# Side-job weight pieces of a hybrid decoder layer on GpSimd's DMA queue instead of SyncE's

## The chip, the cores and the metric

The program runs on one core of one Trainium2 chip. The metric is the time of one execution on the device in microseconds; the shown time is the median of three executions. A profile of one further execution, with every instruction and every DMA packet, is read beside it.

## What is computed

One conditioned decoder layer over 256 tokens of width 2048, in float32. The part that matters here is the first line: a conditioning vector c is multiplied by a large matrix w_ada (2048 x 12288) and gives six vectors that shift, scale and gate the two halves of the layer.

```python
mod = jax.nn.silu(c) @ w_ada + b_ada
shift1, scale1, gate1, shift2, scale2, gate2 = jnp.split(mod[:, None, :], 6, axis=-1)
h = rms_norm(x, norm1_g) * (1.0 + scale1) + shift1
z = h @ w_in + b_in
...
mixed = (g_m[:, :, 0] * y_attn + g_m[:, :, 1] * y_conv) @ w_out
x = x + gate1 * mixed
h2 = rms_norm(x, norm2_g) * (1.0 + scale2) + shift2
return x + gate2 * peer_ffn(h2, peer_w_q, peer_sub_keys, peer_u, peer_v)
```

`y_attn` is a sparse attention with its own output projection, `y_conv` a convolution branch, and `peer_ffn` a product-key expert layer. Nearly all bytes are weights that are read once: 533 MB in 2.5 ms.

## The kernel before

The kernel is one long program for five engines that is written in the order in which TensorE works. **The weight stream** is its spine. A class `Stream` holds a plan of 512 KB chunks (tile `raw`, 128 x 1024, four buffers). `prefetch` issues a chunk's load on SyncE's DMA queue (line 149), ScalarE rounds each half chunk to a high part `hi` (line 153), and VectorE subtracts it to give a low part `lo` (line 159). One half chunk is a piece: `piece` lets TensorE do 12 matmuls of 128 x 256 with it (lines 200 to 202), with `hi` and `lo` made up to three to four pieces ahead (`AHEAD = 3`). A chunk's load can only be issued when the `lo` of the buffer's earlier chunk is done, so SyncE stands at such a wait much of the time.

**Side jobs** are Python generators. After each piece, `step` gives each running job `rate` steps (0.9 means nine steps in ten pieces); what a step emits goes into the engines' queues behind that piece. Two of them read w_ada:

- `ada_steps` (from 418 us to 925 us, beside the attention, the merge of the branches and the output projection) makes shift2, scale2 and gate1. It works through 12 groups of 512 columns, each of 16 pieces of 128 x 512 (256 KB, tile `adaw`, four buffers). Three pieces are asked for ahead; then every step asks for one more and VectorE adds one piece, scaled by c, onto an accumulator `ada` (lines 383 and 385). After the 16th, four steps follow without such a load: TensorE transposes the sums (line 390), ScalarE adds them over the columns (line 394). The rates are 0.7, 0.88, 0.9 and 0.94 in turn; 0.9 and 0.94 hold from the merge on.
- `gate2_steps` (2053 to 2403 us, beside the last expert products, rate 0.25) does the same with 64 pieces (tile `g2w`, line 1289).

Both ask for their pieces on SyncE's queue, so each such load stands in the program order of that queue between two chunks of the stream. GpSimd runs four small memsets at the start and then nothing. At 642 us the same queue also loads x again, one transfer of 2 MB (line 891).

Of the kernel before, what the change touches and what calls it, by code (L numbers as in the profile page):

```python
# [72 lines left out]
def build(nc, tc, d):  # L73
    ctx = ExitStack()
    ve, sc, pe, sp = nc.vector, nc.scalar, nc.tensor, nc.sync
# [34 lines left out]
    def v(name, i=0, n=1):  # L110
        o = VEC[name][0] + i
        return vec[:, o:o + n]
# [248 lines left out]
    def ada_steps(groups, bank):  # L361

        pool = adap[0]
        todo = [(g, k) for g in groups for k in range(KT)]
        ahead = []

        def load():
            if todo:
                g, k = todo.pop(0)
                raw = pool.tile([128, 512], F32, name="adaw", tag="adaw", bufs=4)  # L370
                sp.dma_start(raw, d["w_ada"][k * 128:(k + 1) * 128, (g - 8) * 512:(g - 7) * 512])
                ahead.append(raw)

        for _ in range(3):
            load()
        yield
        for g in groups:
            acc = pool.tile([128, 512], F32, name="ada", tag="ada", bufs=2)
            for k in range(KT):
                load()  # L380
                raw = ahead.pop(0)
                if k == 0:
                    ve.tensor_scalar(acc, raw, sc_c[:, 0:1], None, op0=OP.mult)
                else:
                    ve.scalar_tensor_tensor(acc, raw, sc_c[:, k:k + 1], acc, op0=OP.mult, op1=OP.add)  # L385
                yield
            yield
            ps = bank()
            for j in range(4):
                pe.transpose(ps[:, j], acc[:, j * 128:(j + 1) * 128], ident)  # L390
            yield
            cols = mod[:, 4 * g:4 * g + 4]
            for j in range(4):
                sc.activation(acc[:, j * 128:(j + 1) * 128], ps[:, j], AF.Copy, accum_out=cols[:, j:j + 1])
            yield
            ve.tensor_add(cols, cols, v("b_ada", 4 * g, 4))
            yield
# [881 lines left out]
    def gate2_steps():  # L1279

        todo = [(g, k) for g in range(4) for k in range(KT)]
        ahead = []

        def load():
            if todo:
                g, k = todo.pop(0)
                raw = vp.tile([128, 512], F32, name="g2w", tag="g2w", bufs=4)
                o = D * 3 + g * 512
                sp.dma_start(raw, d["w_ada"][k * 128:(k + 1) * 128, o:o + 512])
                ahead.append(raw)  # L1290

        ve.memset(gacc, 0.0)
        sp.dma_start(gacc[0:1], d["b_gate2"])
        for _ in range(3):
            load()
        yield
        for g in range(4):
            for k in range(KT):
                load()
                a = gacc[:, g * 512:(g + 1) * 512]  # L1300
                ve.scalar_tensor_tensor(a, ahead.pop(0), sc_c[:, k:k + 1], a, op0=OP.mult, op1=OP.add)
                yield
# [130 lines left out]
```

## Time and profile before

| | |
|---|---|
| median of three executions | 2494.17 us (2492.91 to 2499.4) |
| the profiled execution | 2496.72 us, span of its instructions 2494.9 us |
| TensorE busy in that span | 2448.4 us (98%) |
| VectorE, ScalarE busy | 1942.8 us (78%), 1422.5 us (57%) |
| mean granted TensorE clock | 0.995 |
| DMA | 540 MB, 217 GB/s on the mean |

The span runs from the first to the last instruction. A busy share counts time in which at least one instruction of an engine is in work. In views of waits, "A <- B" reads: A stood idle, and the last thing that it waited for was B.

### The profile page before, as it was taken

To read this page: it belongs to the slowest core of one execution; us is meant where nothing else is said; L and a number is where in the kernel's file an instruction comes from. 1 tells how busy PE (TensorE), PEld (TensorE's weight loads), DVE (VectorE), ACT (ScalarE), POOL (GpSimd) and SP (SyncE) were. 2 spreads that over 40 slices of the span, in tenths; PEclk is the share of its full clock that TensorE was granted. 3 is DMA by queue.
4 is the path that set the end of the run, shared out by engine and by line. 5 is a ranking of instruction groups with operands and counts; after the bars stand their busy time and mean duration, and the time that the engine had idled before them with its cause. 6 is when DMAs were issued, how large, how long until landed. Compare 5 with 4: busy or idle time off the path is not lost.

```text
span 2494.9 us, 44063 instructions
## 1 busy us (share of the span) xinstructions
PE 2448.4 (98%) x15324; PEld 2168.3 (87%) x15324; DVE 1942.8 (78%) x4136; ACT 1422.5 (57%) x3198; POOL 0.2 (0%) x4
## 2 busy tenths in 40 slices
PE   7999999999999999999999999999999999999999
PEld 6899999888999899988888888888888888888887
DVE  7979886888787786899997888888655556666665
ACT  1045456776444456555568888887555555555554
POOL 0000000000000000000000000000000000000000
PEclk9999999999999999999999999999999999999999
DMA  9955556655898885555555555555555557777765
GB/s 376 401 195 194 179 191 200 200 156 189 304 296 281 278 292 194 178 191 191 189 189 178 177 177 174 175 177 178 186 193 190 192 193 254 237 242 240 236 209 194
DMA packets 171553, 540.48 MB, mean 217 GB/s; under 512 B 18753, under 2 KB 19009, under 8 KB 171073
## 3 DMA queue, kind: packets, MB, share of 16 engines
q1 hardware_dynamic: 171330, 537.67, 64.5%
q8 instruction: 120, 1.97, 0.3%
q14 instruction: 103, 0.84, 0.1%
HBM read 533.41 MB, written 4.19 MB: 215 GB/s over the span
## 4 chain that ended last, share of the span: by engine, by line
PE 88%; DVE 6%; DMA 5%; issue 1%; SPq 0%; ACT 0%; DVEq 0%
PE ps_acc L213 19%; PE ps_acc L217 9%; PE acc L200 7%; PE acc L202 7%; PE acc L201 7%; DMA adaw<-in_w_ada_dram 4%; DVE acc L309 3%; PE ps_o L1314 2%; PE ps_s L1314 2%; PE ps_t L1314 2%; PE ps_acc L1314 2%; PE ps_o L1313 2%; PE ps_s L1313 2%; PE ps_t L1313 2%; PE ps_acc L1313 2%; PE ps_o L1312 2%
## 5 line engine op out<-in xcount | busy, mean ns | idle before, releaser
L153 ACT CAST hi<-raw 128x512 fp32r<-128x512 f32 x1548 | 952.2, 620 | 808.2 <-PE acc L201 236.8
L159 DVE TENSOR_TENSOR lo<-raw,hi 128x512 fp32r<-128x512 f32 x1548 | 1062.9, 688 | 385.2 <-PE ps_o L1313 78.6
L213 PE MATMUL ps_acc<-h,hi 128*128 128x512 f32 x2048 | 564.6, 397 | 0.0
L213 PEld LDWEIGHTS ps_acc<-h,hi 128*128 128x128 f32 x2048 | 346.7, 188 | 44.2
L217 PEld LDWEIGHTS ps_acc<-h,lo 128*128 128x128 f32 x2048 | 311.4, 188 | 46.4
L200 PE MATMUL acc<-hhi,hi 128*128 128x256 f32 x1200 | 346.9, 289 | 0.0
L202 PE MATMUL acc<-hhi,lo 128*128 128x256 f32 x1200 | 334.7, 279 | 4.3 <-DVE lo L159 4.3
L201 PE MATMUL acc<-hlo,hi 128*128 128x256 f32 x1200 | 334.0, 278 | 0.0
L217 PE MATMUL ps_acc<-h,lo 128*128 128x256 f32 x2048 | 318.0, 277 | 0.0
L200 PEld LDWEIGHTS acc<-hhi,hi 128*128 128x128 f32 x1200 | 226.0, 188 | 6.3 <-issue 5.3
L202 PEld LDWEIGHTS acc<-hhi,lo 128*128 128x128 f32 x1200 | 226.1, 188 | 5.4 <-DVE lo L159 5.3
L201 PEld LDWEIGHTS acc<-hlo,hi 128*128 128x128 f32 x1200 | 226.0, 188 | 3.2 <-issue 3.1
L385 DVE SCALAR_TENSOR_TENSOR ada<-adaw,sc_c,ada 128x512 f32<-128x512 f32 x180 | 134.6, 748 | 49.9 <-DMA adaw<-in_w_ada_dram 49.6
L1204 ACT ACTIVATE Ahi<-ohA,high 128x128 f16<-128x128 f16 x256 | 100.7, 393 | 10.8 <-PE ps_o L1225 10.6
L471 DVE SCALAR_TENSOR_TENSOR cacc<-glu,dwh,cacc 128x256 f32<-128x256 f32 x240 | 105.7, 479 | 0.0
L341 PE MATMUL zb<-hr,w 128*128 128x256 f32 x448 | 101.3, 385 | 0.0
L1204 ACT ACTIVATE Alo<-ohA,low 128x128 f16<-128x128 f16 x256 | 99.0, 387 | 0.0
L341 PEld LDWEIGHTS zb<-hr,w 128*128 128x128 f32 x448 | 85.6, 194 | 11.4
L309 DVE SCALAR_TENSOR_TENSOR acc<-wa,sc_c,acc 128x256 f32<-128x256 f32 x224 | 91.3, 478 | 0.0
L202 PE MATMUL acc<-ohi,lo 128*128 128x256 f32 x256 | 74.2, 290 | 5.2 <-DVE lo L159 4.8
L202 PE MATMUL acc<-mhi,lo 128*128 128x256 f32 x256 | 73.9, 288 | 1.5 <-DVE lo L159 1.5
L201 PE MATMUL acc<-mlo,hi 128*128 128x256 f32 x256 | 73.2, 286 | 1.0 <-DVE mlo L907 1.0
(367 smaller groups left out, 4406.0 us busy)
## 6 DMA issues: line engine op xcount, KB each, us to landing
raw<-in_u_dram SPq DMA_DIRECT2D x256, 512.0 KB, 3.6
raw<-in_v_dram SPq DMA_DIRECT2D x256, 512.0 KB, 4.5
raw<-in_w_in_dram SPq DMA_DIRECT2D x150, 512.0 KB, 4.4
adaw<-in_w_ada_dram SPq DMA_DIRECT2D x192, 256.0 KB, 5.4
wa<-in_w_ada_dram SPq DMA_DIRECT2D x64, 512.0 KB, 8.8
raw<-in_nsa_out_dram SPq DMA_DIRECT2D x32, 512.0 KB, 5.3
raw<-in_w_out_dram SPq DMA_DIRECT2D x32, 512.0 KB, 5.2
raw<-in_peer_wq_dram SPq DMA_DIRECT2D x32, 512.0 KB, 3.7
```

The lines of the kernel that those rows point to most:

```text
L153: sc.copy(hi, self.source(n))
L159: ve.tensor_sub(lo, self.source(n), hi.bitcast(F32))
L200: pe.matmul(ps, hi[:, o:o + 128], xhi[:, k], start=(k == 0), stop=False)
L201: pe.matmul(ps, hi[:, o:o + 128], xlo[:, k], start=False, stop=False)
L202: pe.matmul(ps, lo[:, o:o + 128], xhi[:, k], start=False, stop=(k == nk - 1))
L213: pe.matmul(ps.rearrange("p a t -> p (a t)"), hi[:, o:o + 128], x[:, k].rearrange("p a t -> p (a t)"), start=(k == 0), stop=False)
L217: pe.matmul(ps[:, 1], lo[:, o:o + 128], x[:, k, 0], start=False, stop=(k == nk - 1))
L309: ve.scalar_tensor_tensor(a, raw[:, i], c, a, op0=OP.mult, op1=OP.add)
L341: pe.matmul(zb[n // 2][:, n % 2], ws[k][n // 7][:, n % 7], hr[k], start=(k == 0 and n % 2 == 0), stop=(k == KT - 1), skip_group_check=True)
L1204: sc.activation(part[:, j], A[:, j], AF.Copy, scale=g[:, t0 + j:t0 + j + 1])
L1313: pe.matmul(ps, chi, lo, start=False, stop=False)
L1314: pe.matmul(ps, clo, hi, start=False, stop=(i1 == NK - 1))
```

## The change

The two lines that issue the pieces of w_ada for the side jobs name another engine's queue. Nothing else is different.

```diff
@@ ada_steps @@
                 raw = pool.tile([128, 512], F32, name="adaw", tag="adaw", bufs=4)
-                sp.dma_start(raw, d["w_ada"][k * 128:(k + 1) * 128, (g - 8) * 512:(g - 7) * 512])
+                nc.gpsimd.dma_start(raw, d["w_ada"][k * 128:(k + 1) * 128, (g - 8) * 512:(g - 7) * 512])
                 ahead.append(raw)
@@ gate2_steps @@
                 o = D * 3 + g * 512
-                sp.dma_start(raw, d["w_ada"][k * 128:(k + 1) * 128, o:o + 512])
+                nc.gpsimd.dma_start(raw, d["w_ada"][k * 128:(k + 1) * 128, o:o + 512])
                 ahead.append(raw)
```

The rows of TensorE, VectorE and ScalarE stand in the same order as before. On SyncE's queue in the merge, before, around the load of x (`x_7756`), the pieces `adaw` stand between the stream's chunks `raw`:

```order
L149 DMA raw<-in_w_in_dram 128x1024
L371 DMA adaw<-in_w_ada_dram 128x512
L149 DMA raw<-in_nsa_out_dram 128x1024
L891 DMA x_7756<-in_xT_dram 128x4096
L149 DMA raw<-in_nsa_out_dram 128x1024
L149 DMA raw<-in_w_in_dram 128x1024
L371 DMA adaw<-in_w_ada_dram 128x512 x2
L149 DMA raw<-in_w_in_dram 128x1024
L371 DMA adaw<-in_w_ada_dram 128x512 x2
```

The same place of SyncE's queue in the changed kernel:

```order
L149 DMA raw<-in_w_in_dram 128x1024 x2
L149 DMA raw<-in_nsa_out_dram 128x1024
L891 DMA x_7756<-in_xT_dram 128x4096
L149 DMA raw<-in_nsa_out_dram 128x1024
L149 DMA raw<-in_w_in_dram 128x1024 x2
L149 DMA raw<-in_nsa_out_dram 128x1024 x2
```

The chunks and the load of x keep their order, and nothing stands between them any more. GpSimd's queue, in the changed kernel, from the program's start, with what each row waits for (`DMASW` and `DMAHW` are completions of DMAs of GpSimd's and SyncE's queue, `DVE` is VectorE's progress):

```order
L1424 MEMSET const-uint8-127 128x1
L1429 UNCONDITIONAL_BRANCH [waits barrier_Pool_Activation_PE_DVE_SP_gather]
L371 DMA adaw<-in_w_ada_dram 128x512 [waits DMAHW3_49,DMAHW4_49,DMAHW1_49,DMAHW5_49,DVE_49,Activation_49]
L371 DMA adaw<-in_w_ada_dram 128x512 x3
L371 DMA adaw<-in_w_ada_dram 128x512 [waits DMASW0_49,DVE_49]
L371 DMA adaw<-in_w_ada_dram 128x512 [waits DMASW1_49,DVE_49]
L371 DMA adaw<-in_w_ada_dram 128x512 [waits DMASW2_49,DVE_49]
```

All 192 loads of `adaw` and then the 64 of `g2w` moved here. The first waits for the memory under its buffer, which the program's first stage uses; the next three wait for nothing; from the fifth on each waits for an earlier load and for VectorE's use of the buffer, and for no chunk of the stream.

## Rows read from the trace of the kernel before

**Rows 1.** Page, first line
```profile
span 2494.9 us, 44063 instructions
```
**Rows 2.** Busy time by stretch; columns in the second line
```profile
core 0: us, PE busy (x) PEld busy (x) DVE busy (x) ACT busy (x) POOL busy (x), PEclk, DMA share, GB/s
...
620.00:700.00 80.00, 76.86 (x625) 75.37 (x625) 60.76 (x104) 38.34 (x82) 0.00 (x0) 0.96 0.87 297
700.00:740.00 40.00, 37.80 (x321) 36.78 (x321) 33.37 (x57) 18.94 (x40) 0.00 (x0) 1.00 0.93 301
740.00:930.00 190.00, 175.48 (x1439) 171.74 (x1437) 150.58 (x263) 91.78 (x211) 0.00 (x0) 0.98 0.88 284
930.00:1040.00 110.00, 110.00 (x930) 109.65 (x929) 81.47 (x191) 67.20 (x135) 0.00 (x0) 1.00 0.58 194
2050.00:2400.00 350.00, 350.00 (x1531) 287.18 (x1530) 240.60 (x382) 177.67 (x319) 0.00 (x0) 1.00 0.73 240
```
**Rows 3.** Waits of TensorE, 620 to 930 us: us, times, longest
```profile
PE acc L202 <- DVE lo L159: 10.4, 11, 2.7
PE ps_t L390 <- DVE ada L385: 8.1, 6, 2.1
```
**Rows 4.** Waits of VectorE, 620 to 930 us
```profile
DVE ada L385 <- DMA adaw<-in_w_ada_dram: 49.2, 47, 5.5
```
**Rows 5.** Waits of VectorE, 700 to 930 us
```profile
DVE ada L385 <- DMA adaw<-in_w_ada_dram: 35.5, 39, 2.2
```
**Rows 6.** Timeline of VectorE: start, us, instruction, idle before and its end
```profile
700.92 0.75 DVE L385 SCALAR_TENSOR_TENSOR ada<-adaw,sc_c,ada 128x512 f32<-128x512 f32 x1 [1.31 <-DMA adaw<-in_w_ada_dram]
701.59 0.69 DVE L159 TENSOR_TENSOR lo<-raw,hi 128x512 fp32r<-128x512 f32 x1
...
709.11 0.75 DVE L385 SCALAR_TENSOR_TENSOR ada<-adaw,sc_c,ada 128x512 f32<-128x512 f32 x1 [0.37 <-DMA adaw<-in_w_ada_dram]
```
**Rows 7.** Timeline of SyncE's queue at the same place
```profile
702.30 0.33 SPq L149 DMA_DIRECT2D raw<-in_w_in_dram  x1
702.68 0.91 SPq L371 DMA_DIRECT2D adaw<-in_w_ada_dram  x2
```
**Rows 8.** Line 371, 700 to 930 us: issues in ns, and landing
```profile
L371 SPq DMA_DIRECT2D adaw<-in_w_ada_dram x100: 327/423/684, 702.7 to 919.1; - x100
...
DMA to landing us min/median/max: 4.5/5.8/7.3
```
**Rows 9.** Line 371, two loads that were issued singly
```profile
L371 SPq DMA_DIRECT2D adaw<-in_w_ada_dram x1: 431/431/431, 710.9 to 710.9; - x1
...
DMA to landing us min/median/max: 4.5/4.5/4.5
...
L371 SPq DMA_DIRECT2D adaw<-in_w_ada_dram x1: 424/424/424, 722.2 to 722.2; - x1
...
DMA to landing us min/median/max: 5.1/5.1/5.1
```
**Rows 10.** Tile adaw over the whole span
```profile
L371 SPq DMA_DIRECT2D adaw<-in_w_ada_dram x192: 327/423/1667, 418.2 to 919.1; - x192
...
L383 DVE TENSOR_SCALAR ada<-adaw,sc_c x12: 478/482/486, 423.0 to 895.5; 128x512 f32<-128x512 f32 x12
```
**Rows 11.** Tile g2w, 64 loads of the same size: landing
```profile
DMA to landing us min/median/max: 2.8/5.0/8.6
```
**Rows 12.** Line 149, 700 to 930 us: who waited for chunks, and landing
```profile
  ACT hi L153: 8.1, 6
...
DMA to landing us min/median/max: 3.9/5.2/7.0
```
**Rows 13.** Timeline of SyncE's queue around the load of x
```profile
642.65 0.42 SPq L891 DMA_DIRECT2D x<-in_xT_dram  x1
...
647.54 1.68 SPq L371 DMA_DIRECT2D adaw<-in_w_ada_dram  x2
```
**Rows 14.** Timeline of VectorE after it
```profile
657.42 0.75 DVE L385 SCALAR_TENSOR_TENSOR ada<-adaw,sc_c,ada 128x512 f32<-128x512 f32 x1 [5.50 <-DMA adaw<-in_w_ada_dram]
```

## The prediction

> **What bounds the kernel now.** I read the busy time by stretch first. TensorE is without a gap from 930 to 1040 us and in the last expert products from 2050 to 2400 us, but not in the merge and the output projection, from 620 to 930 us [rows 2]. There it stands idle for 80 - 76.86 = 3.1, 40 - 37.80 = 2.2 and 190 - 175.48 = 14.5 us, together 19.9 us. In two of the three stretches its granted clock is also below 1, so for a part of the time it ran at the lower of its two levels (1.2 GHz for 2.4): 0.96 over 80 us and 0.98 over 190 us are 3.2 + 3.8 = 7.0 us of full clock lost. The stake is therefore 26.9 us, 1.1% of the time; everywhere else that the change touches, TensorE has nothing to get back.
>
> Next the waits there. TensorE waits for VectorE alone: for `lo` of the stream, and, at a group's end, for the accumulator `ada` [rows 3]. VectorE in turn has one large wait, for the pieces `adaw`: 49.2 us in 47 waits [rows 4]. It works in order, so while it stands at an `ada` whose piece has not landed, the `lo` behind it is late too, and with it TensorE.
>
> The timelines tell why a piece is late. The buffer that VectorE frees at 700.92 + 0.75 = 701.67 us is the next piece's [rows 6]. But SyncE first has a chunk to issue, and that waits for the `lo` that ends at 701.59 + 0.69 = 702.28; the chunk goes at 702.30, the piece at 702.68, 1.01 us after its buffer was free [rows 7]. A second piece goes right behind it. The first is used at 709.11, after 0.37 us of idle time: 6.4 us under way. Over 100 loads the median landing is 5.8 us [rows 8], while two that were issued singly took 4.5 and 5.1 [rows 9], mean 4.8: the chunk and the twin ahead on the queue cost about a microsecond more.
>
> With four buffers the loop of one buffer is: freed, issued, landed, used. Before, that is 1.01 + 5.8 + 0.75 = 7.56 us for four steps. TensorE's own pace comes from the undisturbed stretch: 110 us for 930 matmuls are 0.118 us each, 1.42 us for a piece of 12 [rows 2], and at a mean rate of 0.92 steps a piece 1.42 / 0.92 = 1.54 us a step, 6.2 us for four. The loop is 1.36 us too long. In a group of 16 pieces with three asked for ahead, the 4th, 8th, 12th and 16th pay it: 5.4 us. The trace has 35.5 us of this idle time between 700 and 930 us [rows 5], and 100 loads [rows 8] are 6.25 groups: 5.7 us a group, so the loop explains it. TensorE's idle time there is 16.7 us, 2.7 a group. So about 3.0 us a group stay hidden in the three pieces of lead and in the four steps without a load.
>
> **What the change removes.** The wait of `adaw` behind chunks and the issue of the twin: 1.01 us for the first of a pair. VectorE's, ScalarE's and TensorE's rows are the same, so what is left on SyncE is the stream alone; its chunks lose the pieces ahead of them. The 256 issues of 0.42 us leave that queue [rows 10]; SyncE waits for `lo` anyway, so I cost this at nothing.
>
> **What it adds.** GpSimd issues 256 loads. It does nothing else, so nothing is queued behind them but the next load. The trace has no DMA from GpSimd, so its extra time per load from free buffer to landing, call it p, has to be bounded. Below: 0, as quick as SyncE. Above: 2.8 us, one more of the shortest landings of a transfer of this size [rows 11], as if the issue cost as much as the whole transfer. SyncE's own issues of this shape take 0.42 us at the median and 1.67 at the longest [rows 10]; I take the middle of these, p = 1.0.
>
> **What it moves.** GpSimd does not follow the order of the stream. At a group's end, where the program asks for nothing during four steps, it loads as soon as a buffer is free. So four pieces, not three, wait at a group's start, and only the 5th, 9th and 13th pay. It also loads the first four pieces long before 418 us, where TensorE has hardly a gap; I count nothing for that. The pieces of `g2w` are off the path with either queue, as TensorE is busy for 350.00 of 350 us there [rows 2]: nothing to gain or to lose.
>
> At the load of x, 2 MB go onto the queue at 642.65, two pieces behind it at 647.54 [rows 13], and VectorE stands for 5.50 us [rows 14]. On a queue of their own the pieces are not behind x in order, only beside it. This is part of the stake above.
>
> **The sum.** The new loop is p + 4.8 + 0.75 = 5.55 + p, with the single loads' landing since pieces no longer go in pairs behind a chunk. With p = 1.0 it is 6.55 us, 0.35 too long, times three 1.1 us a group, under the 3.0 that stay hidden. By this the whole stake would come back. But groups differ (one wait of 5.5 us beside many of about 1), and at full pace TensorE asks for more bytes than the 284 to 301 GB/s with DMA engines 0.88 to 0.93 busy [rows 2], so landings will not all be 4.8. I keep a third of the stake as lost: 26.9 x 2/3 = 18 us. The profiled execution took 2496.72 us (span 2494.9 [rows 1] and 1.8 around it) and would come to 2478.7; it lies 2.55 us over the median of the runs, so I forecast **2476 us**.
>
> The ends: with p = 0 the loop is 5.55 us, inside 6.2, and the whole stake comes back: 2494.2 - 26.9 = 2467. With p = 1.67, 7.22 us, 1.02 x 3 = 3.1 a group, still about hidden, but any scatter shows; half the stake, 2481. With p = 2.8, 8.35 us, 2.15 x 3 = 6.5 a group, 0.75 more than the 5.7 of today; with 135 loads or 8.4 groups after 620 us that is 6.3 us, and 7.0/19.9 more for the clock, 8.5 in all: 2503. The change turns to a loss where 3 x (p + 5.55 - 6.2) exceeds 5.7, at p = 2.55.
>
> The Trainium skill ("DMA: Bandwidth & Descriptors", section "Specifications") gives a first byte after about 1 us on GpSimd's path and about 0.6 us on SyncE's. By that, as an estimate, p is 0.4 and the sum the full stake, 2467. No run here shows it.
>
> **Rivals.** *No change: the queue was not the limit.* All transfers share the same 16 DMA engines, busy for 0.87 to 0.93 of these stretches against 0.58 behind them [rows 2]. If landings stay at 5.8 us because the engines are full, the new loop is 1.0 + 5.8 + 0.75 = 7.55, as long as the old; three payments instead of four are left as a gain, against chunks that now lose turns to the pieces. Chunks land after 5.2 us at the median and 7.0 at most, against some six pieces or 8.5 us between a buffer's release and the next rounding, and ScalarE already waits 8.1 us for them [rows 12]. The two about cancel: 2490, within 2487 to 2501. Against it speaks that single loads in the same stretch land in 4.8. Beside this stands the Trainium skill's "DMA: Bandwidth & Descriptors", section "Issuing engines are not separate DMA queues": transfers of all issuing engines interleave on the same engines, and a second issuer saves only issue time. The trace shows one queue, so it neither agrees nor disagrees.
>
> *Slower: GpSimd's issue itself is long.* Its place is between a freed buffer and the first byte, 192 times in a row. From p = 2.55 on it decides; 2.8 gives 2503.
>
> *Slower by more: VectorE holds GpSimd's issue up.* If GpSimd could prepare a transfer only while VectorE is idle, which is 190 - 150.58 = 39 of 190 us or 0.21 [rows 2], 1.0 us of issue would stretch to 4.8; the loop would be 10.35, 4.15 x 3 = 12.5 us a group, 6.8 more than today, 57 us in 8.4 groups and 20 for the clock: 2571. Nothing in the trace speaks for it or against it.
>
> The Trainium skill's "SBUF — State Buffer" ("Who interferes with whom") has such a lock, but only for VectorE's two-port modes, and says that a tensor_tensor has none. By that only the 12 scalings of 0.482 us, in the shape of [rows 10], could hold a transfer up, 6 us in all and most of them hidden.
>
> **How the numbers follow.** I give the forecast (2466 to 2487) 0.60, no change (2487 to 2501) 0.18, the long issue (2501 to 2510) 0.12, the lock (above 2510) 0.10. About 0.3%, 7.5 us, is what a measurement of this kernel can tell from no change; so faster has 0.60, same 0.18, slower 0.22. The range for 8 in 10 is 2466 to 2505: it leaves out a few hundredths below and about 0.15 above. The likeliest case's own range is 2466 to 2487.
>
> **What would show it.** Right: `adaw` loads start within about 0.1 us of the end of the use four before, no longer 1.0; landing counted from there below 6 us; VectorE's wait for `adaw` after 620 us under 20 us instead of 49; TensorE's idle time in 620 to 930 us under 8 us, and its clock at 1.00; the first four loads at about 140 us. Wrong: GpSimd's issues of 2.5 us or more in a row; a wait of ScalarE for chunks of well over 8 us in its place; `lo` or `ada` instructions of VectorE longer than 0.69 and 0.75 us, which would mean that the two engines disturb each other; or any change of TensorE's idle time outside 418 to 930 us.

## The result, and the profile after

The changed kernel takes **2467.28 us** (median of four, 2465.55 to 2469.65). The kernel before took 2493.54 us on the same chip (2491.16 to 2499.4). The ratio is 0.9889, with a 95% interval of 0.9875 to 0.9902: 26 us faster by the medians. The forecast of 2476 us, made from 2494.17, is a ratio of 0.9927 and lies outside this interval. The time is at the foot of the range (2466 to 2505) and at the value given for an issue that costs nothing (2467).

The profiled execution took 2467.69 us. The page's first lines, which answer to [rows 1]:

```profile
span 2465.9 us, 44212 instructions
...
PE 2432.3 (99%) x15324; PEld 2156.2 (87%) x15324; DVE 1941.6 (79%) x4136; ACT 1423.4 (58%) x3198; POOL 139.4 (6%) x260
```

Busy time by stretch, the columns as in [rows 2]:

```profile
418.00:470.00 52.00, 52.00 (x429) 49.80 (x427) 43.21 (x96) 33.05 (x99) 8.59 (x16) 1.00 0.68 224
620.00:700.00 80.00, 79.31 (x688) 78.72 (x687) 68.22 (x117) 40.86 (x89) 21.49 (x40) 1.00 0.93 328
700.00:740.00 40.00, 38.63 (x341) 38.44 (x340) 34.93 (x62) 21.19 (x51) 10.20 (x19) 1.00 0.93 322
740.00:930.00 190.00, 186.01 (x1581) 185.05 (x1580) 158.29 (x278) 105.78 (x233) 40.28 (x75) 1.00 0.87 300
```

TensorE's idle time in the three stretches of the stake fell from 19.9 us to 0.69 + 1.37 + 3.99 = 6.05 us, and the granted clock is at full speed in all of them (it was 0.96, 1.00 and 0.98). More bytes move per second there (300 to 328 GB/s for 284 to 301), since the same work is done in less time.

The waits of three engines from 620 to 930 us (us, times, longest), which answer to [rows 3, 4]:

```profile
DVE ada L385 <- DMA adaw<-in_w_ada_dram: 22.4, 33, 1.9
ACT hi L153 <- DMA raw<-in_w_in_dram: 13.4, 12, 2.1
ACT hi L153 <- DMA raw<-in_nsa_out_dram: 8.3, 7, 2.5
...
PE ps_t L390 <- DVE ada L385: 4.7, 3, 2.5
...
PE acc L202 <- DVE lo L159: 0.8, 3, 0.5
```

VectorE's wait for the pieces halved (49.2 to 22.4 us). TensorE's wait for `lo`, which stood behind it, nearly vanished (10.4 to 0.8), and that for `ada` at a group's end went from 8.1 to 4.7. The longest wait, 5.5 us at the load of x, is gone; the longest is now 1.9.

One loop of a buffer in the timelines, first VectorE's rows, then GpSimd's:

```profile
720.04 0.75 DVE L385 SCALAR_TENSOR_TENSOR ada<-adaw,sc_c,ada 128x512 f32<-128x512 f32 x1
```
```profile
721.08 0.54 POOL L371 DMA_DIRECT2D adaw<-in_w_ada_dram  x1 [1.17 <-DVE ada L385]
```

The use ends at 720.79, the load is issued at 721.08, 0.29 us later. This replaces the 1.01 us of [rows 6, 7], and here no chunk and no twin stand between. Line 371 from 700 to 930 us (durations of the issues in ns), which answers to [rows 8]:

```profile
L371 POOL DMA_DIRECT2D adaw<-in_w_ada_dram x94: 536/538/545, 700.7 to 888.8; - x94
...
  DVE ada L385: 17.0, 25
...
DMA to landing us min/median/max: 3.8/5.5/7.5
```

**Where the time came from.** Both programs give TensorE the same instructions in the same order, so the start of its n-th instruction can be compared between the two traces. Of the 29.0 us between the two profiled executions, 25.5 came in 620 to 930 us. 1.15 us came at 418 us, where the first four pieces, loaded at 137 us, are now waiting for VectorE. Another 1.9 us came between 150 and 200 us, in the first stage. That step is there too in e2_gate_only below, which leaves `adaw` where it was, and missing in e4_pool_five, which has the change; so it belongs to the single execution, and the medians differ by 26.3 us. The rest, some 0.5 us, came in small parts before 418 us. From 930 us to the end nothing came or went, the stretch of gate2 included.

### The profile page after: what moved, and what is told of

Same layout as the page of the kernel before. It is cut to its first block, busy times and chain, and to the rows that moved or that the text cites. A ratio compares the mean times of both kernels' runs of the same rounds, so it can differ in the third digit from the quotient of the medians.

```text
span 2465.9 us, 44212 instructions
## 1 busy us (share of the span) xinstructions
PE 2432.3 (99%) x15324; PEld 2156.2 (87%) x15324; DVE 1941.6 (79%) x4136; ACT 1423.4 (58%) x3198; POOL 139.4 (6%) x260
## 4 chain that ended last, share of the span: by engine, by line
PE 88%; DVE 6%; DMA 3%; issue 2%; POOL 0%; SPq 0%; ACT 0%; DVEq 0%; POOLq 0%
PE ps_acc L213 19%; PE ps_acc L217 10%; PE acc L200 8%; PE acc L202 7%; PE acc L201 7%; DVE acc L309 3%; DMA adaw<-in_w_ada_dram 3%; PE ps_o L1312 2%; PE ps_s L1312 2%; PE ps_t L1312 2%; PE ps_o L1314 2%; PE ps_s L1314 2%; PE ps_acc L1312 2%; PE ps_t L1314 2%; PE ps_acc L1314 2%; PE ps_o L1313 2%
## 5 line engine op out<-in xcount | busy, mean ns | idle before, releaser
L385 DVE SCALAR_TENSOR_TENSOR ada<-adaw,sc_c,ada 128x512 f32<-128x512 f32 x180 | 134.4, 746 | 22.9 <-DMA adaw<-in_w_ada_dram 22.4
L371 POOL DMA_DIRECT2D adaw<-in_w_ada_dram x192 | 104.8, 546 | 784.1 <-DVE ada L383 333.5
L1289 POOL DMA_DIRECT2D g2w<-in_w_ada_dram x64 | 34.3, 537 | 1429.3 <-ACT hi L153 864.7
L1204 ACT ACTIVATE Ahi<-ohA,high 128x128 f16<-128x128 f16 x256 | 100.7, 393 | 10.9 <-PE ps_o L1225 10.7
L200 PE MATMUL acc<-mhi,hi 128*128 128x256 f32 x256 | 73.2, 286 | 0.0
```

The costliest lines, as they stand in the source:

```text
L200: pe.matmul(ps, hi[:, o:o + 128], xhi[:, k], start=(k == 0), stop=False)
L1204: sc.activation(part[:, j], A[:, j], AF.Copy, scale=g[:, t0 + j:t0 + j + 1])
```

## The experiments

My theory ahead of them: a buffer's loop (freed, issued, landed, used) was longer than the four steps it may take, and the change shortens it by issuing as soon as the buffer is free. The rivals: the queue of its own is worth something by itself; or running ahead at group ends does it; or gate2's pieces or GpSimd's path have a part. All times are medians beside runs of the kernel before on the same chip.

| run | us | kernel before | ratio, 95% |
|---|---|---|---|
| e1_ada_only | 2470.34 | 2496.80 | 0.9898 (0.9879 to 0.9917) |
| e2_gate_only | 2495.26 | 2496.80 | 0.9994 (0.9984 to 1.0003) |
| e3_sync_five | 2467.01 | 2493.04 | 0.9889 (0.9872 to 0.9905) |
| e4_pool_five | 2461.21 | 2493.04 | 0.9874 (0.9857 to 0.9890) |
| e5_pool_coupled | 2529.49 | 2496.80 | 1.0135 (1.0114 to 1.0155) |
| e6_pool_delay | 2481.53 | 2493.04 | 0.9947 (0.9931 to 0.9964) |
| e7_pool_delay2 | 2496.91 | 2496.80 | 1.0001 (0.9987 to 1.0014) |
| e8_act_queue | 2470.69 | 2493.04 | 0.9902 (0.9886 to 0.9919) |
| e9_coupled_pad | 2495.27 | 2495.67 | 1.0000 (0.9990 to 1.0009) |
| e10_shift | 2526.18 | 2495.67 | 1.0122 (1.0105 to 1.0139) |
| e11_ahead_only | 2492.62 | 2495.67 | 0.9982 (0.9971 to 0.9992) |
| e12_early_only | 2473.03 | 2495.67 | 0.9905 (0.9888 to 0.9921) |

### Each half of the change alone: e1_ada_only, e2_gate_only

The first moves only `adaw` to GpSimd's queue, the second only `g2w`.

> Only the adaw loads go to GpSimd's queue, the g2w loads stay with SyncE. Theory (the whole gain comes from adaw, which no longer waits behind chunks of the stream): 2467 us, the same as the full change, within 0.2%. Rival (relieving SyncE's queue helps wherever it is done, gate2 too): between 2470 and 2485.

> Only the g2w loads go to GpSimd's queue. Theory: 2494 us, no change, as TensorE has no gap from 2050 to 2400 us. Rival: a part of the gain, some 5 to 10 us, or a loss of some us if GpSimd's issues disturb VectorE there.

The pieces of `adaw` alone give 0.9898, within the interval of the full change. Its 2470.34 us also touch the foot of the rival's range (2470 to 2485), so the other half decides: the pieces of `g2w` give nothing. Under gate2, TensorE stays without a gap in e2_gate_only, as in [rows 2]:

```profile
2050.00:2400.00 350.00, 350.00 (x1531) 287.20 (x1530) 240.56 (x383) 177.73 (x318) 32.19 (x60) 1.00 0.73 236
```

### A longer loop allowed, without any other queue: e3_sync_five; and with it: e4_pool_five

Both have five buffers instead of four, and four pieces asked for ahead. The memory comes from a second buffer of `mr`, a tile of the merge. The first keeps all loads on SyncE's queue, the second has the change as well.

```diff
-                raw = pool.tile([128, 512], F32, name="adaw", tag="adaw", bufs=4)
+                raw = pool.tile([128, 512], F32, name="adaw", tag="adaw", bufs=5)
...
-        for _ in range(3):
+        for _ in range(4):
...
-            mr = tp.tile([128, T], F32, name="mr", tag="mr", bufs=2)
+            mr = tp.tile([128, T], F32, name="mr", tag="mr", bufs=1)
```

> The kernel before with all loads on SyncE's queue, but five adaw buffers and four pieces asked for ahead (the memory comes from the tile mr, one buffer instead of two). Theory of the loop: 7.56 us now stand against five steps, 7.7 us, so the waits nearly go without any change of queue: 2465 to 2472. Rival (the pieces' place on SyncE's queue itself is what costs, or the DMA engines are full): 2480 to 2494.

> The changed kernel with five adaw buffers and four pieces asked for ahead. Theory: a loop of 6.5 us against 7.7, so the 6 us that TensorE still stands idle between 620 and 930 us go too: 2460 to 2463. Rival (the DMA engines, 0.87 to 0.93 busy, set the pace by now): 2466 to 2469, with longer landings.

One more buffer on the old queue has the whole gain of the change (0.9889 both). The pieces are then issued as late as before and land later, after 6.3 us at the median, but they have five steps for it (line 371, 700 to 930 us):

```profile
L371 SPq DMA_DIRECT2D adaw<-in_w_ada_dram x95: 327/425/1582, 702.4 to 887.6; - x95
...
DMA to landing us min/median/max: 4.6/6.3/7.4
```

From the end of a use to the issue it is 0.80 us on the mean, and the loop is 0.80 + 6.30 + 0.75 = 7.85 us, about the five steps of 7.7 that the expectation named; of the 34.0 us that e4_pool_five wins in 620 to 930 us, 6.9 stay lost. From 930 us on, TensorE's instructions in both runs go at the pace of the kernel before to 0.02 us, so the smaller `mr` costs nothing there.

With both edits TensorE has no gap left from 620 to 930 us (here the last stretch of e4_pool_five, and VectorE's wait, which was 49.2 us):

```profile
740.00:930.00 190.00, 190.00 (x1623) 190.00 (x1622) 163.06 (x291) 112.58 (x243) 39.70 (x74) 1.00 0.87 301
```
```profile
DVE ada L385 <- DMA adaw<-in_w_ada_dram: 2.1, 4, 1.3
```

This has the lowest median of the kernels run. Its interval overlaps that of the changed kernel (0.9857 to 0.9890 beside 0.9875 to 0.9902), but by TensorE's instructions it gained 34.0 us in 620 to 930 us, 8.5 more than the changed one. With no gap and full clock left, 34.0 us is what there was to win; the changed kernel took 25.5 of it.

### The issue made late again: e6_pool_delay, e7_pool_delay2

GpSimd fills the buffer with zeros before it issues the load, once or twice, which adds time between the free buffer and the issue and leaves the queue its own.

```diff
+                nc.gpsimd.memset(raw, 0.0)
                 nc.gpsimd.dma_start(raw, d["w_ada"][k * 128:(k + 1) * 128, (g - 8) * 512:(g - 7) * 512])
```

> The changed kernel, but GpSimd fills each adaw buffer once with zeros before it issues the load: some 0.5 to 0.8 us more between free buffer and landing. Theory of the loop: 7.1 to 7.3 us, about 3 us a group, just at what stays hidden: 2470 to 2477. Rival (only the four pieces at a group's start count): 2467 to 2469.

> The changed kernel, but GpSimd fills each adaw buffer twice with zeros once it is free, before it issues the load: a dearer issue, some 1 to 1.5 us more between free buffer and landing. Theory of the loop (6.5 us in the changed kernel against 6.2, three payments a group, 3.0 us hidden): 7.8 us, 1.6 x 3 = 4.8 us a group, about 1.8 us of it on TensorE, 8.4 groups and the clock: 2482 to 2490. Rival (the length of the issue does not matter, four pieces that wait at a group's start are the whole gain): 2467 to 2471.

e6_pool_delay kept less than half of the gain, e7_pool_delay2 none; both lost more than expected. GpSimd's timeline in e6_pool_delay shows the delay: 0.53 us of work and 0.30 us until the issue.

```profile
716.70 0.53 POOL L371 MEMSET adaw<- 128x512 f32 x1 [0.24 <-DVE ada L386]
717.52 0.54 POOL L372 DMA_DIRECT2D adaw<-in_w_ada_dram  x1 [0.30 <-POOL adaw L371]
```

So a loop that is half a microsecond longer costs more than half of the gain (11.6 us are left of 25.5 in 620 to 930 us): the loop has hardly any room.

The run also limits what the early issue explains. On the mean its loads go out 0.95 us after the buffer is free, later than the 0.78 of the kernel before, and yet the 11.6 us are kept. What is left in its favour is that it runs ahead at a group's end and that its loads land after 5.40 us instead of 5.79; how much each of the two is worth was not separated.

### GpSimd's queue, coupled to the stream: e5_pool_coupled, e9_coupled_pad; and what disturbed the first: e10_shift

Before each load GpSimd copies one element of the `lo` for which SyncE would have waited there, so that the load stands behind a chunk's `lo` again, but on a queue of its own. The copy goes into a new tile `touch`, of 4 bytes in e5_pool_coupled.

```diff
+    touch = const.tile([128, 1], F32, name="touch")
...
+                lo = S.parts.get(2 * S.loaded - 9)
+                if lo is not None:
+                    nc.gpsimd.tensor_copy(touch, lo[1][:, 0:1].bitcast(F32))
```

> The changed kernel, but GpSimd reads one element of the stream's latest lo before each adaw load, so that the load waits for what it waited for on SyncE and cannot run ahead at a group's end; the DMA queue stays its own. Theory (going ahead of the stream is what counts): from free buffer to issue about 1 us again for the first of two, the loop 0.7 us longer than in the changed kernel (7.2 to 7.5 us), four payments a group, VectorE's wait for adaw back to 40 to 50 us and the time to 2485 to 2495. Rival (a queue of its own is what counts, as pieces no longer stand behind a chunk): 2467 to 2472, with the wait near 20 us.

It came out slower than the kernel before, by 33 us, which no theory had. TensorE's instructions show why this says little: in 620 to 930 us it is within 2 us of the kernel before, and the 33 us are lost in every other stage from 200 us on (4.3 from 1040 to 1300 us, 4.7 from 1300 to 1640). The tile moves every buffer allocated after it by 4 bytes. e10_shift is the kernel before with that tile alone, written once; e9_coupled_pad is e5_pool_coupled with a tile of 256 bytes.

> The kernel before with one more buffer of 4 bytes a partition, written once with zeros, ahead of nearly all other buffers; queues and order unchanged. Theory (the 4 bytes cost what the coupled run lost outside 620 to 930 us, about 33 us): 2520 to 2530. Rival (the 4 bytes cost nothing, the coupled run lost it by its reads): 2494.

> As the coupled run (GpSimd reads one element of the stream's latest lo before each adaw load), but the target of that read is a buffer of 256 bytes a partition in place of 4, so that the buffers allocated after it keep their alignment. Theory (going ahead of the stream is the gain, and what the coupled run lost outside 620 to 930 us came from buffers that lay 4 bytes off): no loss outside that stretch, the gain inside it gone, 2488 to 2498 us. Rival (the reads themselves disturb VectorE or TensorE): 2520 to 2530 again.

e10_shift lost 30 us by 4 bytes of memory (below, in the last section), stage by stage nearly what e5_pool_coupled lost outside 620 to 930 us. With 256 bytes the loss is gone and e9_coupled_pad is as fast as the kernel before. Its stretch looks like that of [rows 2]:

```profile
740.00:930.00 190.00, 175.94 (x1422) 171.50 (x1421) 149.78 (x261) 90.61 (x210) 76.77 (x160) 0.97 0.85 282
```

So a queue of its own gives nothing when the issue is held behind the stream and made later by a copy. The reserve matters: within a group the loads of e9_coupled_pad went out 1.22 us after the buffer was free, on the mean, for 0.78 before, and landed after 5.48 us for 5.79, so that the whole loop is about the old one. A coupled load with the old delay wasn't run; if it landed as soon, the rule in the table below would give it some 10 us (an estimate: 0.78 + 5.48 + 0.75 = 7.01 us against 7.32). That the queue alone is worth nothing is therefore not shown.

### Another queue: e8_act_queue

The pieces go on ScalarE's DMA queue (`sc.dma_start`), where each issue waits in ScalarE's own order.

> The kernel before with the adaw loads on ScalarE's DMA queue: again a queue of its own, but an engine whose order holds the hi of the stream too. Theory (not standing in an order with the stream is what counts): ScalarE meets the load behind a hi that waits for TensorE, and while a load waits for its buffer the next hi waits too; 2475 to 2500. Rival (a queue of its own is enough): 2467 to 2472.

The expectation missed: 0.9902 is as good as GpSimd's queue within the intervals. The waits of ScalarE (first row) and TensorE from 620 to 930 us:

```profile
ACT hi L153 <- DVE ada L385: 17.5, 18, 3.0
...
PE ps_t L390 <- DVE ada L385: 3.5, 2, 2.9
...
PE acc L202 <- DVE lo L159: 1.5, 5, 0.5
```

ScalarE does stand at the pieces' buffers, 17.5 us, as expected. But it works three to four pieces ahead of TensorE, and the wait probably goes up in that lead; no run shows this by itself. The landing is 5.5 us at the median on both queues, so no difference of path shows there.

### Early issue and running ahead apart: e11_ahead_only, e12_early_only

The coupling of e9_coupled_pad for some loads alone: in e11_ahead_only for all but a group's first (`load(k > 0)` coupled), in e12_early_only for the first alone, which stops GpSimd from loading during the four steps at a group's end.

> As the coupled run with the 256-byte buffer, but the first load within a group does not read lo, so GpSimd may still load the fourth piece ahead at a group's end; the other loads wait for the stream's lo as on SyncE. Theory of the loop: about 7.3 us but three payments in place of four, 3.3 us a group, a little over the 3.0 that stay hidden: 2475 to 2485, between the full change and the fully coupled run. Rival (the quick issue alone is the gain): as fully coupled, 2488 to 2498.

> The other half: only the first load within a group reads lo, so the fourth piece cannot be loaded ahead at a group's end, all others go as soon as their buffer is free. Theory of the loop: 6.54 us with four payments, 1.4 us a group, hidden: 2467 to 2472. Rival (four pieces that wait at a group's start are the gain): 2480 to 2495.

e11_ahead_only missed its expectation and lies in the rival's range. It is 2.65 us faster than e9_coupled_pad, with intervals that touch; by TensorE's instructions it gains 1.7 us on that run in 620 to 930 us and 1.4 at 418 us, and in 620 to 930 us nothing on the kernel before. So running ahead is worth some 3 us by itself, hardly clear of the noise. e12_early_only has 22.6 us of the change's 26.3: most of the gain comes with loads that go out early within a group. It missed its upper bound by a microsecond; running ahead adds about 4 us on top of an early issue.

## Why the prediction was too high

**The stretch, the wait and the loop were right.** The gain came from 620 to 930 us, through VectorE's wait for `adaw`. `g2w` is worth nothing, as costed (e2_gate_only), and so, as far as it shows, is SyncE's relief: e3_sync_five has the same time without it.

**The step that failed is the size of what comes back:** "I keep a third of the stake as lost: 26.9 x 2/3 = 18 us". Measured, it is 34.0 x 3/4 = 25.5 us. Two things are wrong in it. *The stake*: I read it from idle time and granted clock (19.9 + 7.0); e4_pool_five, without a gap, won 34.0 in that stretch. The missing 7.1 us lay inside TensorE's busy time. In e4_pool_five the records give a matmul of line 202 some 279 ns, while the next one starts after 116, so the first 0.16 us of a stop still count as busy. Start by start against e4_pool_five, the 34.0 us of the kernel before are 19.9 us of idle time in 22 stops, 3.5 us of the same stops that count as busy, 6.0 us at the lower clock, 3.5 us in 38 stops too short to show as idle, and 1.1 us in differences below 30 ns. *The share*: a quarter of it, 8.5 us, stayed lost, not a third. The first makes 7.1 x 2/3 = 4.7 us, the second 34.0 x (3/4 - 2/3) = 2.8, and with the 1.15 us at 418 us, which I counted as nothing, these are the 8.7 us between 2476 and 2467.3.

**"About 3.0 us a group stay hidden"** came from the same short stake. With 34.0 us in 8.4 groups TensorE lost 4.0 us a group, the clock included, and not 2.7, so of VectorE's 5.7 only 1.7 were hidden. In the changed kernel it is alike: VectorE waits 17.0 us over 94 loads or 5.9 groups, 2.9 a group, where I had 1.1; TensorE loses 8.5 / 8.4 = 1.0 of them.

**The loop's sum was right by two errors that cancel.** The table takes, from the records of the loads from 700 to 930 us, one by one, the mean time from the end of the use that frees a buffer to the issue, and from the issue to the landing, without the first load after a group's end. The changed kernel's loop is 6.65 us; I had put p + 4.8 + 0.75 = 6.55. The issue was quicker than p = 1.0, but landings did not fall to the 4.8 of two single loads: the engines stay 0.87 to 0.93 busy and the mean landing is 5.57. Counted as the prediction defines it, p is 0.33 + 5.57 - 4.8 = 1.10, but 0.77 of it is landing and only 0.33 GpSimd's delay. For the kernel before I had 7.56, as I took the delay of the first of a pair for all; on the mean it is 7.32.

The 4.8 was a misreading of the trace of the kernel before. Both of its loads, at 710.9 and 722.2 us, stand directly behind a chunk, and a later load that was issued in the same way, at 752.4 us, took 6.3:

```profile
710.49 0.33 SPq L149 DMA_DIRECT2D raw<-in_nsa_out_dram  x1
710.87 0.43 SPq L371 DMA_DIRECT2D adaw<-in_w_ada_dram  x1
```
```profile
L371 SPq DMA_DIRECT2D adaw<-in_w_ada_dram x1: 427/427/427, 752.4 to 752.4; - x1
...
DMA to landing us min/median/max: 6.3/6.3/6.3
```

From 700 to 930 us the loads of the kernel before that were issued singly and whose landing is recorded (32) took 5.7 us on the mean, those issued in pairs (52) 5.85. The microsecond that the prediction put down to the chunk and the twin ahead on the queue was not there.

What the loop costs can be put together from the prediction's numbers, after the runs and with none fitted to them: its excess over 6.2 us, times 8.4 groups, times four payments where the load after a group's end is late (it went out 3.5 to 7.2 us after its buffer was free) and three where it is early (0.3 to 1.7 us; up to 4.3 in e7_pool_delay2). Beside it stands the loss that TensorE's instructions show in 620 to 930 us, counted from e4_pool_five:

| kernel | freed to issue, landing, use: us | payments | by the rule, us | measured, us |
|---|---|---|---|---|
| before | 0.78 + 5.79 + 0.75 = 7.32 | 4 | 37.6 | 34.0 |
| changed | 0.33 + 5.57 + 0.75 = 6.65 | 3 | 11.3 | 8.5 |
| e12_early_only | 0.36 + 5.56 + 0.75 = 6.67 | 4 | 15.8 | 12.3 |
| e6_pool_delay | 0.95 + 5.40 + 0.75 = 7.10 | 3 | 22.7 | 22.4 |
| e11_ahead_only | 1.23 + 5.41 + 0.75 = 7.39 | 3 | 30.0 | 34.2 |
| e7_pool_delay2 | 2.13 + 4.67 + 0.75 = 7.55 | 3 | 34.0 | 38.5 |
| e9_coupled_pad | 1.22 + 5.48 + 0.75 = 7.45 | 4 | 42.0 | 35.9 |
| e8_act_queue | 0.12 + 5.44 + 0.75 = 6.31 | 4 | 3.7 | 10.2 |

The rule gives 37.6 - 11.3 = 26.3 us for the change where 25.5 were measured, and no row is more than 6.5 us off; e1_ada_only (11.3 by the rule, 10.7 measured) and e2_gate_only (41.0, 36.7) fit alike. It is a description and no proof. It lets nothing stay hidden, while in the changed kernel VectorE waits 2.9 us a group where the rule has 0.45 x 3 = 1.35 and TensorE loses 1.0. And the step at full pace, between uses within a group of e4_pool_five from 620 to 930 us, is 1.60 us, so that four take 6.4 and not 6.2; with 6.4 the change comes to 24.6 us, but the rows of e6_pool_delay, e7_pool_delay2 and e11_ahead_only fall short by 5 to 10. e8_act_queue is the farthest; whether ScalarE's own waits are what it pays beside the loop was not tried. In e7_pool_delay2 the landing falls to 4.67 as the issues come later, which by the rule is why two fills cost little more than e9_coupled_pad's copy.

**The rivals.** *No change, since chunks lose turns.* Its mechanism is there but does not decide: ScalarE's wait for chunks of w_in and the branch's weights went from 4.7 + 8.4 = 13.1 us to 13.4 + 8.3 = 21.7 in 620 to 930 us. The rows of the kernel before:

```profile
ACT hi L153 <- DMA raw<-in_nsa_out_dram: 8.4, 4, 3.8
ACT hi L153 <- DMA raw<-in_w_in_dram: 4.7, 5, 1.4
```

From 700 to 930 us chunks land later than in [rows 12]:

```profile
  ACT hi L153: 10.0, 9
...
DMA to landing us min/median/max: 4.3/5.9/8.3
```

Of TensorE's waits in the stretch only 0.8 us are for `lo`, so little of this lateness reached it. The rival's other half, landings at 5.8 us on full engines, came close (5.57), and the single loads of 4.8 that were held against it were the misreading above; its error was p = 1.0. *A long issue*: GpSimd's take 0.54 us, and from 700 to 930 us all loads but one start 0.9 us or more after the load before them. *VectorE holds GpSimd up*: no. GpSimd's issues take 536 to 545 ns whatever VectorE does, and landings are no longer than before. The two instructions of VectorE that run beside the loads are as long as before, 0.69 and 0.75 us (VectorE's groups, 700 to 930 us: busy us, mean ns):

```profile
L159 DVE TENSOR_TENSOR lo<-raw,hi 128x512 fp32r<-128x512 f32 x156 | 105.7, 686 | 16.8 <-PE ps_o L202 4.6 <-PE acc L202 4.6 <-issue 3.2
L385 DVE SCALAR_TENSOR_TENSOR ada<-adaw,sc_c,ada 128x512 f32<-128x512 f32 x92 | 68.7, 747 | 17.3 <-DMA adaw<-in_w_ada_dram 17.0
```

The Trainium skill ("DMA: Bandwidth & Descriptors", section "Rules for kernel authors") says that spreading transfers over SyncE, ScalarE and GpSimd does not help bandwidth and saves only the sequencers' issue time. e9_coupled_pad agrees as far as it goes (ratio 1.0000, with the reserve named there). In this case the gain did not lie in issue time (0.54 us on GpSimd for 0.42 on SyncE): in a queue that issues in order a load also waits out its neighbours' semaphores, 1.01 us for the first of a pair [rows 6, 7] and 0.29 now (0.78 and 0.33 on the mean), and being rid of that was most of 1.1% here; the landing, 5.79 and 5.57 us, has a smaller part.

**The list of signs.** The issue came 0.29 us after the use, not 0.1; VectorE's wait is 22.4 us, just over the 20 named; the landing counted from the freed buffer is 5.85 us at the median, just under 6; TensorE's idle time is 6.05 us, under 8, and its clock is at 1.00; the first four loads start at 137 us. ScalarE's wait for chunks, a sign of wrong, rose from 8.1 to 10.0 us from 700 to 930 us without a loss that shows.

## What to carry to other kernels

Before moving a load to another queue, write down the loop of one buffer (freed, issued, landed, used) and the steps it may take; what exceeds them is paid for once per turn, and either an earlier issue or one more buffer pays it back (0.9889 each here, 0.9874 together). A queue that issues in order holds a load behind the waits of its neighbours, and that was most of what moving it removed. Don't take the latency of a transfer from two records when the trace has eighty. Don't take the stake from idle rows alone, as the start of every stop counts as busy, and don't call a wait hidden because the idle rows are shorter than it: a run that takes the wait away altogether tells what it cost.

## What the runs showed of the hardware that I had not expected

Four bytes of memory cost 30 us. In e10_shift the only edit is a tile of 4 bytes a partition, ahead of other buffers, and one write to it:

```diff
+    touch = const.tile([128, 1], F32, name="touch")
+    ve.memset(touch, 0.0)
```

TensorE's busy time in the whole span went from 2448.4 to 2480.4 us for the same instructions; VectorE's and ScalarE's stayed within 3 us. The matmuls of line 217 show it, in TensorE's groups from 1040 to 1640 us (busy us, mean ns), first in the kernel before, then in e10_shift:

```profile
L217 PE MATMUL ps_acc<-h,lo 128*128 128x256 f32 x1655 | 257.2, 277 | 0.0
```
```profile
L217 PE MATMUL ps_acc<-h,lo 128*128 128x256 f32 x1628 | 259.4, 282 | 0.0
```

TensorE has no gap there in either, and from start to start of these matmuls it is 114.7 ns before and 118.9 in e10_shift, so the loss is in the matmuls' own pace. Over the whole program line 217 lost 8.6 us and line 1312 11.3, of 29.0 us. In e9_coupled_pad, with 256 bytes, line 217 is at 277 and 114.7 ns again, and e5_pool_coupled, which has the 4 bytes and not the `memset`, is at 118.9. In 620 to 930 us alone e10_shift gained 5.1 us; why is open. Whether another size of shift also costs, and which operand's place matters, was not tried.
